# Output projection's inputs split by groups beside the last input projection, and gate and up products issued in turns

## The chip, the cores and the metric

The kernel runs on one core of a Trainium2 chip. TensorE (PE) multiplies matrices and also loads the stationary operand (PEld); VectorE (DVE), ScalarE (ACT) and GpSimd (POOL) do elementwise work; transfers from and to device memory are issued by SyncE (SP), a few by ACT and POOL, and run on 16 DMA engines. The metric is the device time of one execution in microseconds; lower is better. Each engine works through its own queue in order.

## The reference

One block of a diffusion transformer over 512 tokens of width 1024, with 256 context tokens, all in float32. Cut to what the change touches:

```python
def token_mix(h, w_in_l, w_out_l, ...):
    q, zf_f, zf_b, i, g, gate_b, gate_c, v = split_proj(h @ w_in_l)       # w_in: 1024 x 4096
    o_hg, s_f, s_b = hgrn2_mix(q, i, zf_f, zf_b, g, ...)                  # 4 heads, normalised, times silu(g)
    u = gate_c * v
    y = gate_b * dwconv3(u, conv_l)                                       # 3 taps along the grid row
    return jnp.concatenate([o_hg, y], axis=-1) @ w_out_l, s_f, s_b        # w_out: 1024 x 1024

def expert_choice_ffn(h, w_router, w_gate, w_up, w_down):                 # 16 experts, 64 tokens each
    aff = jax.nn.softmax(h @ w_router)
    gate, idx = lax.top_k(aff.T, cap)
    xs = h[idx]
    hid = silu(xs @ w_gate) * (xs @ w_up)                                 # 1024 -> 2048, per expert
    return zeros.at[idx].add((hid @ w_down) * gate)                       # 2048 -> 1024

def reference(...):
    x = x + g1 * mx            # mx: output of token_mix
    hx2 = modulate(rms_norm(x, norm_ffn), sh2, sc2)
    x = x + g2 * expert_choice_ffn(hx2, ...)
    return rms_norm(x, norm_final)
```

## The kernel before

It has three stages. **Input projections and heads**: the 1024 x 4096 projection runs section by section. Since the plain float32 product is slow, each operand is split into a rounded part (hi, made by ACT) and a rest (lo, made by DVE), and three products are summed: hi*hi, hi*lo, lo*hi (`split_w` L264, `products` L286). Between the sections the four recurrent heads are worked off (`scores`, `head_sum`, `head_gate`). The result, 1024 features by 512 tokens, stands in `mixed`: four rows of 128 features from the heads (k = 0 to 3, written by `head_gate` L576) and four from the convolution (k = 4 to 7, written by `keep_gb` L599). The last section is the second half of `gate_b`; its last product feeds `keep_gb(3)`, and `head_gate(3)` follows it.

**Output projection and routing**: `out_weights` (L754) loads `w_out` in four pieces of 1 MB (columns 0 to 511 and 512 to 1023, features 0 to 511 and 512 to 1023), multiplies the second column half by `g1b` on POOL (L761) and splits each piece into `wo_hi` (ACT, L764) and `wo_lo` (DVE, L765). `mix_parts` (L747) splits `mixed` for one block of 128 tokens into `m` (ACT L751, DVE L752). `residual` (L783) multiplies one token block by one column half: 24 matmuls (L792 to L794), for k = 0 to 7 hi*hi, hi*lo, lo*hi. Then come the sum with x, a transpose (L805), the router's logits (L810), and for each block the softmax and the running top 64 of each expert (`affinity`, `top`), the last of it on DVE alone.

**Experts**: 16 experts in 8 pairs. Each expert's `w_gate` and `w_up` come in 8 pieces each of 1 MB (128 rows by 2048), each pair's two `w_down` in 16. 64 tokens fill only half of PE's columns, so the gate products write to rows 0 to 63 of a PSUM bank and the up products to rows 64 to 127 (`hidden` L969, matmuls L979); four banks `gu` hold 2048 columns. Each float32 matmul of the program is two in the trace, and so four pairs per piece are 16 matmuls of L979 in the trace. After them the banks are copied (L989), transposed (`ht`, L994), multiplied into `hid` (L998), and go through `w_down` (`y`, L1033), the gates (L1005) and the scatter (`po`, L1011). Weights are streamed through `ring_a` (4 slots of 1 MB; the pieces of `w_in` and `w_out` go through it too) and, from the third stage on, 13 more (`ring_b`) and four lent ones. A load is issued in the program's order on SP and waits until the matmuls that read its slot are done; up to eight loads are under way at a time.

The order on each engine is set by the Tile scheduler, which places what is ready by the program's order, or earlier by `tc.high_priority(offset=300)` (300 instructions earlier in rank); `tc.issue_after(ins)` puts what the block traces on the engine of `ins` behind `ins` in its queue, without a wait for it to end. In the program so ordered, ACT's queue behind the last head's small steps holds: `wo_hi` of columns 512 to 1023 (first piece), `wo_hi` of columns 0 to 511 (both), `m` for the four token blocks, `wo_hi` of columns 512 to 1023 (second piece). The first of these is written over `h_hi`, which the last projection's matmuls read. PE's queue holds the gate and up products of expert 0 in turns (gate, up, gate, up, ...); from the middle of expert 1 on it holds, piece by piece, the eight gate products in a row and then the eight up products; of 512 gate products of the program 73 are followed at once by the up product of the same bank.

Tiles of a stage are laid over those of stages that are over, and each waits for the last reader of what lies under it. `wo_hi` of columns 0 to 511 lies over the heads' buffers, `wo_lo` over the heads' buffers with the last head's normalised output `on` and the begin of `vtok`, `m_0` and `m_1` over the rest of `vtok`, the states and the queries; `m_2`, `m_3` and the second column half over `sig`, `h_hi`, `h_lo` and the split weights.

## Time and profile before

| | |
|---|---|
| median of 3 runs | 1326.99 us (1326.15 to 1328.63) |
| profiled execution | 1325.83 us, of which the span is 1324.0 us |
| instructions | 15074 |
| PE busy | 1259.7 us (95%) |
| DVE, ACT, POOL busy | 407.2, 231.4, 42.6 us |
| read from device memory | 455.73 MB, 346 GB/s over the span |
| chain that ended last | PE 85%, issue 9%, DVE 4%, ACT 2%, DMA 1% |

The profile is one execution. A row of the timeline has the start, the duration, the engine, the line, the operation, what is written from what is read, and a count; in brackets stands how long the engine stood idle before it and what ended that. Rows of windows give, for each stretch, its length, the busy time of each engine with its number of instructions, the granted TensorE clock (1.00 is 2.4 GHz, 0.50 is 1.2 GHz), the share of the DMA engines and GB/s. A busy PE isn't PE at its peak: matmuls overlap, and a row merges neighbours of one kind.

### The profile page before, as it was taken

The numbers are of one execution on the slowest core, as the hardware profiler recorded it, in microseconds if no ns is written. First come the engines' busy times: TensorE is split into PE (matmuls) and PEld (weight loads), VectorE is DVE, ScalarE is ACT, GpSimd is POOL, SyncE is SP. The second block draws the span as 40 slices with busy tenths as digits, with TensorE's granted clock in tenths as the row PEclk, the third lists the DMA queues.
The fourth block names the chain that finished last, engine by engine and source line by source line (L and its number), as shares of the span: only waits on it lengthen the run. The fifth ranks groups of instructions, "written<-read, shape, count | busy, mean of one in ns | idle before, by whom it ended". The sixth has DMA issues, their size and how long they took to land.

```text
span 1324.0 us, 15074 instructions
## 1 busy us (share of the span) xinstructions
PE 1259.7 (95%) x6250; PEld 680.4 (51%) x6250; DVE 407.2 (31%) x843; ACT 231.4 (17%) x473; POOL 42.6 (3%) x47
## 2 busy tenths in 40 slices
PE   5999999998969999999999999999999999999995
PEld 3688988876834344444444444444444444444432
DVE  5557667885452111112111111211121121011113
ACT  4422554524311000000100000010000001000012
POOL 1000031140000000000000000000000000000000
PEclk9999999998979999999999999999999999999998
DMA  9567622218389999999999999999999999999993
GB/s 370 205 224 258 207 76 89 71 38 312 142 356 398 407 427 373 412 426 427 427 426 427 426 427 426 426 427 427 427 426 427 426 427 427 426 427 426 424 407 133
DMA packets 94608, 458.83 MB, mean 347 GB/s; under 512 B 7245, under 2 KB 21690, under 8 KB 47434
## 3 DMA queue, kind: packets, MB, share of 16 engines
q1 hardware_dynamic: 93360, 454.06, 84.1%
q0 software_dynamic: 992, 3.74, 0.8%
q8 instruction: 49, 0.80, 0.2%
q14 instruction: 21, 0.17, 0.0%
q10 hardware_dynamic: 186, 0.06, 0.0%
HBM read 455.73 MB, written 2.10 MB: 346 GB/s over the span
## 4 chain that ended last, share of the span: by engine, by line
PE 85%; issue 9%; DVE 4%; ACT 2%; DMA 1%; POOLq 0%; DVEq 0%; POOL 0%; ACTq 0%
PE gu L979 36%; PE y L1033 15%; PE pg L937 5%; PE px L290 3%; PE px L291 3%; PE px L295 3%; PE po L1011 3%; PE ht L994 2%; PE wo L792 1%; PE wo L794 1%; PE wo L793 1%; PE pi L406 1%; PE pi L407 1%; PE pi L405 1%; PE px_f L324 1%
## 5 line engine op out<-in xcount | busy, mean ns | idle before, releaser
L979 PE MATMUL gu<-wg,shared 128*64 128x512 f32 x1024 | 465.8, 600 | 0.7 <-ACT gs L989 0.7
L979 PE MATMUL gu<-wu,shared 128*64 128x512 f32 x1024 | 462.8, 599 | 0.0
L1033 PE MATMUL y<-wd,hid 128*64 128x512 f32 x896 | 209.2, 595 | 0.0
L979 PEld LDWEIGHTS gu<-wg,shared 128*64 128x64 f32 x1024 | 127.5, 136 | 154.6 <-issue 149.1
L979 PEld LDWEIGHTS gu<-wu,shared 128*64 128x64 f32 x1024 | 128.7, 136 | 136.0 <-issue 135.2
L1033 PEld LDWEIGHTS y<-wd,hid 128*64 128x64 f32 x896 | 81.4, 137 | 112.1 <-issue 108.5
L989 DVE COPY gs<-gu 128x512 f32<-128x512 f32 x32 | 22.0, 691 | 321.0 <-PE gu L979 321.0
L937 PEld LDWEIGHTS pg<-pool_a,x 128*128 128x128 f32 x512 | 62.4, 195 | 40.7 <-issue 35.0
L1005 DVE SCALAR_TENSOR_TENSOR yt<-y,gate,g2b 128x512 f32<-128x512 f32 x16 | 12.0, 750 | 217.2 <-PE y L1033 193.4
L290 PE MATMUL px<-h_hi,whi 128*128 128x512 f32 x192 | 76.9, 400 | 0.0
L989 ACT COPY gs<-gu 128x512 f32<-128x512 f32 x32 | 18.7, 587 | 331.7 <-PE gu L979 331.7
L295 PE MATMUL px<-h_hi,wlo 128*128 128x512 f32 x192 | 75.3, 392 | 0.0
L291 PE MATMUL px<-h_lo,whi 128*128 128x512 f32 x192 | 74.9, 390 | 0.0
L937 PE MATMUL pg<-pool_a,x 128*128 128x128 f32 x512 | 71.8, 289 | 1.6 <-DVE pool_a L929 1.6
L940 ACT ACTIVATE shared<-pg,b,a 128x128 f32<-128x128 f32 x32 | 14.6, 458 | 295.9 <-PE pg L937 295.9
L943 DVE TENSOR_SCALAR shared<-pg,a,b 128x128 f32<-128x128 f32 x32 | 13.1, 410 | 132.1 <-PE pg L937 132.1
L283 DVE TENSOR_TENSOR wlo<-wi,whi 128x1024 fp32r<-128x1024 f32 x28 | 38.8, 1384 | 27.0 <-ACT whi L282 27.0
L1011 PE MATMUL po<-yhl,g 128*128 128x512 f32 x128 | 40.4, 427 | 5.9 <-ACT yhl L1006 5.9
L1006 ACT CAST yhl<-yt 128x512 fp32r<-128x512 f32 x16 | 9.9, 618 | 193.3 <-DVE yt L1005 193.3
L1011 PEld LDWEIGHTS po<-yhl,g 128*128 128x128 f32 x128 | 21.5, 188 | 41.4 <-ACT yhl L1006 13.8
L608 DVE SCALAR_TENSOR_TENSOR adas<-wa,shared,adas 128x512 f32<-128x512 f32 x56 | 41.4, 747 | 1.4 <-DMA wa<-in_w_ada 0.4
L994 PE MATMUL ht<-ident,gs 128*128 128x128 f32 x256 | 34.9, 279 | 6.9 <-DVE hid L998 6.9
(315 smaller groups left out, 1326.1 us busy)
## 6 DMA issues: line engine op xcount, KB each, us to landing
wg<-in_w_gate SPq DMA_DIRECT2D x128, 1024.0 KB, 18.4
wu<-in_w_up SPq DMA_DIRECT2D x128, 1024.0 KB, 15.6
wd<-in_w_down SPq DMA_DIRECT2D x120, 1024.0 KB, 15.3
wa<-in_w_ada SPq DMA_DIRECT2D x22, 1024.0 KB, 6.5
wi<-in_w_in SPq DMA_DIRECT2D x16, 1024.0 KB, 5.2
wd<-in_w_down SPq DMA_DIRECT2D x16, 512.0 KB, 10.4
wo<-in_w_out SPq DMA_DIRECT2D x4, 1024.0 KB, 5.3
xt<-in_x SPq DMA_DIRECT2D x2, 1024.0 KB, 6.7
```

The lines of the kernel that those rows point to most:

```text
L283: dve.tensor_tensor(lo, v, hi.bitcast(F32), op=ALU.subtract)
L290: mm(px, hi[:, k], h_hi[:, k], start=f, stop=False)
L291: mm(px, hi[:, k], h_lo[:, k], start=False, stop=False)
L295: mm(px, lo[:, k], h_hi[:, k], start=False, stop=l)
L608: dve.scalar_tensor_tensor(acc, ts[k // 4][:, (k % 4) * 512:(k % 4 + 1) * 512], cs[:, k, 0:1], acc, op0=ALU.mult, op1=ALU.add)
L937: mm(pg[:, :P], x1[:, tb, k * P:(k + 1) * P], ohr[:, tb], start=tb == 0, stop=tb == NT - 1)
L940: act.activation(xs[:, k], pg[:, :P], AF.Identity, scale=a2[:, k, 0:1], bias=b2[:, k, 0:1])
L979: mm(gu[n][i * CAP:(i + 1) * CAP], xs[:, k, ssl], w[:, n * 512:(n + 1) * 512], start=k == 0, stop=k == KD - 1, skip_group_check=True)
L989: (act.copy if n % 2 else dve.tensor_copy)(to, fr)
L994: pe.transpose(pt[:, i * P:(i + 1) * P], gs[:, f * P:(f + 1) * P], ident)
L1011: mm(po, g[:, tb * P:(tb + 1) * P], yhl[:, i, nsl], start=first and i == 0, stop=i == 1)
L1033: mm(y[n][i * CAP:(i + 1) * CAP], hid[:, i, f], wd[i][:, s, n * 512:(n + 1) * 512], start=f == 0, stop=f == DFF // P - 1, skip_group_check ...
```

## The change

It has three parts.

1. The inputs of the output projection. `mix_parts` and `out_weights` are ranked 300 instructions earlier for token block 0 and columns 0 to 511, and block 0 is split by groups of k: 0 to 2, 4 to 6, then 3 and 7, so that the first two need neither `head_gate(3)` nor `keep_gb(3)`. `head_gate(3)` is ranked earlier too. The second `wo_lo` piece is queued behind `keep_gb(3)` on DVE. Token blocks 1 to 3 follow, and the casts of columns 512 to 1023 are queued on ACT behind the last cast of `m`. In the first `residual` the 24 matmuls are ordered by the groups: hi*hi and lo*hi of k 0 to 2, hi*lo of these, then hi*hi and lo*hi of the other groups, and hi*lo of those last.
2. The tiles' places. On the left side the order was `wo_hi`, `wo_lo`, `m_0`, `m_1`; it becomes `wo_hi`, `m_0`, `m_1`, `wo_lo`. So `m_0` lies over the heads' buffers, `m_1` over `on` and the begin of `vtok`, and `wo_lo` over `vtok`, states and queries.
3. Gate and up products. Each L979 product is queued behind the one before it in the program's order, through all experts, so they go gate, up, gate, up.

The same sums are made from the same products; in the first `residual` they are added in another order.

```diff
     def keep_gb(i, px):
-        dve.tensor_tensor(cy[i], cy[i], px, op=ALU.mult)
+        mixed_last.append(dve.tensor_tensor(cy[i], cy[i], px, op=ALU.mult).ins)
...
-    head_gate(HEADS - 1)
+    with tc.high_priority(offset=PRIO):
+        head_gate(HEADS - 1)
...
+    groups = [slice(0, 3), slice(4, 7), slice(3, 8, 4)]
+
+    def mix_parts(tb, ks):
         src = mixed[:, ks, tb * P:(tb + 1) * P]
-        act.copy(mix[tb][:, 0, ks], src)
+        ins = act.copy(mix[tb][:, 0, ks], src)
         dve.tensor_tensor(mix[tb][:, 1, ks], src, mix[tb][:, 0, ks].bitcast(F32), op=ALU.subtract)
+        return ins
+
+    def out_weights(n, q):
+        raw = stream(w_out[0, q * 512:(q + 1) * 512, n * 512:(n + 1) * 512]
+                     .rearrange("(k p) n -> p k n", p=P), f"wo_{n}_{q}")
+        rv = raw.rearrange("p (k n) -> p k n", k=4)
+        if n:
+            gp.tensor_tensor(rv, rv, g1b[:, n * 512:(n + 1) * 512].unsqueeze(1)
+                             .to_broadcast([P, 4, 512]), op=ALU.mult)
+        hi, lo = (t[:, 4 * q:4 * q + 4] for t in wo[n])
+        act.copy(hi, rv)
+        return lambda: dve.tensor_tensor(lo, rv, hi.bitcast(F32), op=ALU.subtract)
...
+    wo[0] = [p_out.tile([P, KD, 512], F32R, name="wo_hi_0")]
+    for tb in range(NT):
+        mix[tb] = (p_out if tb < 2 else late).tile([P, 2, KD, P], F32R, name=f"m_{tb}")
+    wo[0].append(p_out.tile([P, KD, 512], F32R, name="wo_lo_0"))
+    wo[1] = [late.tile([P, KD, 512], F32R, name=f"wo_{q}_1") for q in ("hi", "lo")]
+    with tc.high_priority(offset=PRIO):
+        rest = [out_weights(0, 0)]
+        for g in groups[:2]:
+            mix_parts(0, g)
+        rest.append(out_weights(0, 1))
+        mix_parts(0, groups[2])
+        rest[0]()
+        with tc.issue_after(mixed_last[-1]):
+            rest[1]()
+    for tb in range(1, NT):
+        ready = mix_parts(tb, slice(0, KD))
+    with tc.issue_after(ready.ins):
         for q in range(2):
...
-    out_weights(0, p_out)
-    for tb in range(NT):
-        mix_parts(tb, slice(0, KD), p_out if tb < 2 else late)
-    out_weights(1, late)
+            out_weights(1, q)()
...
-        for k in range(KD):
-            hi, lo = mix[tb][:, 0, k], mix[tb][:, 1, k]
-            mm(po, hi, whi[:, k, nsl], start=k == 0, stop=False)
-            mm(po, hi, wlo[:, k, nsl], start=False, stop=False)
-            mm(po, lo, whi[:, k, nsl], start=False, stop=k == KD - 1)
+        hi, lo = mix[tb][:, 0], mix[tb][:, 1]
+        three = [(hi, whi), (hi, wlo), (lo, whi)]
+        if tb == 0 and c == 0:
+            a, b, d = ([*range(KD)[g]] for g in groups)
+            steps = [(w, k) for ks in (a, b, d) for w in three[::2] for k in ks]
+            steps = steps[:6] + [(three[1], k) for k in a] + steps[6:] + [(three[1], k) for k in b + d]
+        else:
+            steps = [(w, k) for k in range(KD) for w in three]
+        for i, ((m, wt), k) in enumerate(steps):
+            mm(po, m[:, k], wt[:, k, nsl], start=i == 0, stop=i == len(steps) - 1)
...
+    pairwise = []
...
                 for i, w in enumerate((wg, wu)):
-                    mm(gu[n][i * CAP:(i + 1) * CAP], xs[:, k, ssl], w[:, n * 512:(n + 1) * 512],
-                       start=k == 0, stop=k == KD - 1, skip_group_check=True)
+                    with tc.issue_after(pairwise[-1]) if pairwise else nullcontext():
+                        ins = mm(gu[n][i * CAP:(i + 1) * CAP], xs[:, k, ssl],
+                                 w[:, n * 512:(n + 1) * 512], start=k == 0, stop=k == KD - 1,
+                                 skip_group_check=True)
+                    pairwise[:] = [ins.ins]
```

## Rows read from the trace of the kernel before

**Rows 1.** The page: the GB/s that the DMA engines moved in 40 slices of the span, and one line of the DMA issues (count, KB each, median us from issue to landing).

```profile
GB/s 370 205 224 258 207 76 89 71 38 312 142 356 398 407 427 373 412 426 427 427 426 427 426 427 426 426 427 427 427 426 427 426 427 427 426 427 426 424 407 133
...
wg<-in_w_gate SPq DMA_DIRECT2D x128, 1024.0 KB, 18.4
```

**Rows 2.** One pair of experts in the middle of the third stage, from the scatter of one pair to that of the next (606.31 to 722.75): windows of all engines, windows of the L979 products alone, and two pieces of the chain that ended last (start, us, what) inside it.

```profile
606.31:722.75 116.44, 114.82 (x508) 49.84 (x508) 18.79 (x43) 9.07 (x19) 0.00 (x0) 1.00 1.01 427
...
606.31:722.75 116.44, 67.13 (x256) 23.25 (x256) 1.00 1.01 427
...
623.60 5.35 PE gu L979 x16
...
637.38 16.00 PE gu L979 x64
```

**Rows 3.** Expert 0, whose gate and up products go in turns: a window of L979 alone for one piece of each (k = 1), and three of its rows on PE's timeline.

```profile
389.88:393.46 3.58, 3.58 (x16) 1.05 (x16) 1.00 0.93 339
...
391.64 0.59 PE L979 MATMUL gu<-wg,shared 128*64 128x512 f32 x1
391.65 0.59 PE L979 MATMUL gu<-wu,shared 128*64 128x512 f32 x1
392.07 0.59 PE L979 MATMUL gu<-wg,shared 128*64 128x512 f32 x1
```

**Rows 4.** PE's timeline from the last input projection to the output projection.

```profile
295.58 0.39 PE L553 MATMUL o<-s_c,q2d 128*128 128x128 f32 x2
...
301.29 0.60 PE L575 MATMUL pt_o<-ident,on 128*128 128x128 f32 x4
308.04 0.79 PE L792 MATMUL wo<-wo_hi,m 128*128 128x512 f32 x1 [6.15 <-ACT m L751]
```

**Rows 5.** ACT's timeline in that stretch.

```profile
296.01 0.28 ACT L559 ACTIVATE on<-o 128x128 f32<-128x128 f32 x1 [10.46 <-PE o L553]
...
301.54 5.50 ACT L764 CAST wo_hi<-wo 128x2048 fp32r<-128x2048 f32 x3 [3.82 <-PE px L295]
306.95 3.88 ACT L751 CAST m<-mixed 128x1024 fp32r<-128x1024 f32 x4
```

**Rows 6.** DVE's timeline in that stretch.

```profile
298.62 0.69 DVE L568 TENSOR_TENSOR on<-o,or 128x512 f32<-128x512 f32 x1
301.49 0.69 DVE L599 TENSOR_TENSOR mixed<-mixed,px 128x512 f32<-128x512 f32 x1 [2.18 <-PE px L295]
...
303.47 6.69 DVE L765 TENSOR_TENSOR wo_lo<-wo,wo_hi 128x2048 fp32r<-128x2048 f32 x3 [0.70 <-ACT wo_hi L764]
310.09 4.62 DVE L752 TENSOR_TENSOR m<-mixed,m 128x1024 fp32r<-128x1024 f32 x4
```

**Rows 7.** Windows of all engines around the begin of the output projection (after the window and its length: PE, PEld, DVE, ACT, POOL, clock, DMA share, GB/s).

```profile
301.90:308.04 6.14, 0.00 (x0) 0.00 (x1) 5.44 (x5) 6.14 (x5) 0.00 (x0) 0.88 0.35 106
308.04:313.23 5.19, 5.19 (x11) 3.50 (x12) 5.19 (x4) 4.59 (x4) 0.00 (x0) 0.50 1.01 384
313.23:318.50 5.27, 5.27 (x24) 4.37 (x23) 4.53 (x5) 0.00 (x0) 0.00 (x0) 0.99 0.60 197
```

**Rows 8.** SP's timeline: the last load of `w_in`, and the second and third of `w_out`; and ACT's first cast of that last `w_in` piece.

```profile
211.62 0.37 SPq L70 DMA_DIRECT2D wi<-in_w_in  x1
...
244.47 15.88 SPq L70 DMA_DIRECT2D wo<-in_w_out  x2
...
265.47 1.04 ACT L282 CAST whi<-wi 128x1024 fp32r<-128x1024 f32 x1 [1.24 <-PE px L291]
```

**Rows 9.** Windows in the first two pairs of experts in which the DMA engines moved less (columns as in rows 7), and the SP queue's longest total wait from 420 to 600 (us in total, times, longest).

```profile
425.00:435.00 10.00, 10.00 (x56) 4.40 (x54) 2.05 (x8) 1.35 (x3) 0.00 (x0) 1.00 0.83 306
515.00:530.00 15.00, 15.00 (x58) 5.69 (x58) 1.81 (x8) 0.46 (x1) 0.00 (x0) 1.00 0.88 315
545.00:550.00 5.00, 5.00 (x24) 2.01 (x22) 0.00 (x0) 0.00 (x0) 0.00 (x0) 1.00 0.91 351
...
SPq L70 <- PE gu L979: 102.4, 48, 11.1
```

**Rows 10.** The end: windows of 4 us (columns as in rows 7), and PE's timeline from the last up product on.

```profile
1284.00:1288.00 4.00, 4.00 (x20) 1.29 (x18) 0.00 (x0) 0.00 (x0) 0.00 (x0) 1.00 1.05 408
...
1296.00:1300.00 4.00, 4.00 (x17) 1.24 (x18) 3.02 (x5) 1.45 (x4) 0.00 (x0) 1.00 0.33 126
...
1267.57 2.31 PE L979 MATMUL gu<-wu,shared 128*64 128x512 f32 x5
...
1275.19 15.67 PE L1096 MATMUL y<-wd,hid 128*64 128x512 f32 x72
...
1297.30 10.51 PE L1096 MATMUL y<-wd,hid 128*64 128x512 f32 x46
```

**Rows 11.** The beginning of the kernel, where PE works in short bursts: windows of 2 us (columns as in rows 7), and PE's timeline there.

```profile
18.00:20.00 2.00, 1.12 (x5) 0.33 (x4) 0.69 (x1) 1.73 (x2) 0.00 (x0) 1.00 1.05 409
...
26.00:28.00 2.00, 0.89 (x2) 0.79 (x3) 1.21 (x4) 1.66 (x3) 0.00 (x0) 0.66 1.05 409
...
19.75 1.02 PE L215 MATMUL ada_t<-sel,ada_ev 128*128 128x2 f32 x8 [0.88 <-ACT whi L332]
...
27.11 2.08 PE L324 MATMUL px_f<-h_hi,whi 128*128 128x512 f32 x4 [2.22 <-ACT h_hi L309]
```

More of the change, by code (lines that the diff above doesn't have):

```diff
@@ L1 @@
-from contextlib import ExitStack
+from contextlib import ExitStack, nullcontext
 import concourse.bass as bass
@@ L596, in keep_v @@
                                  op0=ALU.mult, op1=ALU.add)
+    mixed_last = []
     def keep_gb(i, px):
-        dve.tensor_tensor(cy[i], cy[i], px, op=ALU.mult)
+        mixed_last.append(dve.tensor_tensor(cy[i], cy[i], px, op=ALU.mult).ins)
     def ada_sum(col0):
@@ L745, in dit_block @@
     mix, wo = {}, {}
-    def mix_parts(tb, ks, pool=None):
-        if pool:
-            mix[tb] = pool.tile([P, 2, KD, P], F32R, name=f"m_{tb}")
+    groups = [slice(0, 3), slice(4, 7), slice(3, 8, 4)]
+    def mix_parts(tb, ks):
         src = mixed[:, ks, tb * P:(tb + 1) * P]
-        act.copy(mix[tb][:, 0, ks], src)
+        ins = act.copy(mix[tb][:, 0, ks], src)
         dve.tensor_tensor(mix[tb][:, 1, ks], src, mix[tb][:, 0, ks].bitcast(F32), op=ALU.subtract)
-    def out_weights(n, pool):
-        wo[n] = [pool.tile([P, KD, 512], F32R, name=f"wo_{q}_{n}") for q in ("hi", "lo")]
-        for q in range(2):
-            raw = stream(w_out[0, q * 512:(q + 1) * 512, n * 512:(n + 1) * 512]
-                         .rearrange("(k p) n -> p k n", p=P), f"wo_{n}_{q}")
-            rv = raw.rearrange("p (k n) -> p k n", k=4)
-            if n:
-                gp.tensor_tensor(rv, rv, g1b[:, n * 512:(n + 1) * 512].unsqueeze(1)
-                                 .to_broadcast([P, 4, 512]), op=ALU.mult)
-            hi, lo = (t[:, 4 * q:4 * q + 4] for t in wo[n])
-            act.copy(hi, rv)
-            dve.tensor_tensor(lo, rv, hi.bitcast(F32), op=ALU.subtract)
@@ L767, in dit_block @@
-    late = tc.alloc_tile_pool(name="late", bufs=1, side="right", reuse_waits="tile")
-    out_weights(0, p_out)
-    for tb in range(NT):
-        mix_parts(tb, slice(0, KD), p_out if tb < 2 else late)
-    out_weights(1, late)
+        return ins
[9 more added lines that the diff above has]
+        return lambda: dve.tensor_tensor(lo, rv, hi.bitcast(F32), op=ALU.subtract)
@@ new lines, in dit_block @@
+    late = tc.alloc_tile_pool(name="late", bufs=1, side="right", reuse_waits="tile")
+    wo[0] = [p_out.tile([P, KD, 512], F32R, name="wo_hi_0")]
[12 more added lines that the diff above has]
+            rest[1]()
```

## The prediction

> **What bounds the kernel now.** First the 40 slices of the span with their GB/s [rows 1]: from the 17th slice on the DMA engines move 426 to 427 GB/s, slice after slice, but before the 13th much less. So the kernel has a first part, where transfers have time, and a second that is a stream of weights. In the second I read one pair of experts [rows 2]. Its period is 116.44 us; PE is busy for 114.82 of it, but the DMA share is 1.01. A pair needs 48 loads of 1.0486 MB (16 gate, 16 up, 16 down), 50.33 MB; at 427 GB/s that is 117.9 us. Both engines are full, and PE's work can't start before its weights land: the transfers are the bound there, PE only just behind. In the first part I read PE's idle time. The largest stretch on PE's own path is the 6.15 us before the first matmul of the output projection, put down to an ACT cast of `m` [rows 4].
>
> **Part 1, the inputs of the output projection.** ACT has nothing to do from 297.72 on (the end of its last row before the gap) and waits 3.82 us for the last projection's product, because the head of its queue, a cast of columns 512 to 1023, is written over `h_hi`; then come three casts of 1.83 each, and only then the cast of `m` at 306.95 [rows 5]. PE could have gone on at 301.9 [rows 4]. After the idle time the granted clock is 0.50 (1.2 GHz): 11 matmuls take 5.19 us, where 24 at 0.99 take 5.27, .22 each [rows 7]. So the cold start costs 5.19 − 11 × .22 = 2.8, and the most that this part can give is 6.15 + 2.8 = 8.9.
>
> What has to be ready. The heads' last product ends at 295.97 [rows 4], so from then on the new places are free; the normalised `on` is written until 299.31 [rows 6], but the tiles of block 0 no longer lie over it. ACT from 297.72: two casts of 1.83, and block 0's `m` (0.97 whole [rows 5], an estimated 1.2 in three parts) make 4.9, to about 302.6; the third part must wait for the two last multiplications, done near 303. DVE from 299.31, where a first `wo_hi` of 1.83 is just there: `wo_lo` 2.23 (6.69 / 3), the multiplications 2 × .69, the parts of `m` an estimated 1.4 (1.16 whole), the second `wo_lo` 2.23, together 7.2, to about 306.5 [rows 6]. PE, starting at 301.9, needs 24 × .22 = 5.3, to 307.2; its order puts the four products that read the second `wo_lo` last, at 306.3. DVE is therefore the tight engine. I put down 1.6 us: some .3 there, up to .6 for the last group, about .7 for block 1, whose DVE part comes at 307.7, and for `wo_lo` of columns 512 to 1023, which is now behind the rest. Gain 8.9 − 1.6 = 7.3. Bounds: 8.9, if nothing waits; about 4, if PE begins near 304.3 and cold again (6.15 − 2.4 = 3.7).
>
> Edits with one answer: the same casts are made, one in three parts (ACT and DVE have the spare time above). The loads of `w_out` are issued earlier on SP and may pass `w_in` there; before, the last `w_in` load is issued at 211.62 and first cast at 265.47, and the next but one `w_out` load at 244.47 [rows 8]: over 50 us of cover against the 18.4 from issue to landing of a load of this size [rows 1]. I cost that at nothing; without the cover it would be such a landing. POOL's multiplications stay with columns 512 to 1023. What is queued behind the added orders: on DVE the second `wo_lo` stands behind the last `gate_b` product, which it must let pass anyway; on ACT the casts of columns 512 to 1023 stand behind the last `m`, near 306 to 307, as against 301.54 and 310.74 for first and last before [rows 5]; the products that read them come after two blocks, 48 × .22 = 10.6 us behind 301.9.
>
> **Part 3, gate and up products.** Rows 0 to 63 and 64 to 127 of a bank are different columns of PE: in turns, the two start .01 us apart and the next gate product .43 after the first [rows 3]. A piece of both then takes 3.58 [rows 3]. In blocks a lone piece takes 5.35, and 64 in a row 16.00, or 4.00 a piece [rows 2]: some up products there run beside gate products of later pieces. Over a pair L979 takes 67.13 for 16 pieces, 4.20 each [rows 2]. All in turns: 16 × 3.58 = 57.3, which is 9.8 less, and PE's period falls from 116.4 to about 106.6, 11.3 below the 117.9 of the transfers.
>
> So the gain is not 8 × 9.8 = 78: it is what the transfers allow. It comes in two places. **Gaps of the stream.** In the first pairs SP's loads wait for PE to release slots (102.4 us in 48 waits; some do no harm, as up to eight loads run at once), and the engines move 306, 315 and 351 GB/s in three windows [rows 9]. Against 427 these lose 10 × 121/427 = 2.8, 15 × 112/427 = 3.9, and 5 × 76/427 = .9, together 7.7. The first is inside expert 0, which has turns already; the other two, 4.8, lie in the blocky part. I take 4, with 0 (another wait keeps the slots) and 7.7 as ends. **The end.** In the window 1296 to 1300 the engines move 126 GB/s x 4 us; at 407 that is 1.24 us, so the last weights land at 1297.24. PE's last down products end at 1307.8, 10.5 later [rows 10]: 46 matmuls, more than the last pieces need. With 10 us less per pair PE has long caught up, and only the last piece's 8 matmuls, .22 each, stand behind the landing: some 2 us. That gives 10.5 − 2 = 8.5. Against it: the last expert's own sequence. Its gate and up products end at 1269.8, its down products begin at 1275.2 and need 128 × .218 = 27.9 with 2.9 of `po` between [rows 10], while the last 16 loads need 41 us: it catches up within about 1. I take 8; bounds 6.5 and 8.6. What follows the last product stays.
>
> One rule speaks against this. What the rows show: PE, once it has caught up, waits about 4.91 − 3.58 = 1.3 us for each piece pair (2 loads / 427 GB/s). Early in the kernel PE works in bursts with waits of .24 to .88, busy 56% to 89%, at clock 1.00; a wait of 2.22 ends at clock .66 and then .50 [rows 11]. By the rows the new waits lie between these, nearer the harmless ones. The Trainium skill, TensorE: Matmul & The Clock Gate, section "HAM oscillation — how this bites in real kernels", says that a kernel whose K-tiles are shorter than the wait for the next slice falls to the low clock and starts every K-tile cold. By that rule each piece would pay the cold start again; our trace has its short waits at full clock, and no run so far shows it here.
>
> **The rivals.**
> (a) *The conversions come late.* A tile of the new layout, or the queue's order, holds a first cast until the `gate_b` product is through; for: the same happened to the head of ACT's queue in before [rows 5]. PE restarts cold near 304.3: 3.7 instead of 7.3, giving about 1310.
> (b) *Turns are hidden by the transfers everywhere.* The gaps stay and the tail is set by something else; against: the 46 matmuls after the last landing are PE's own backlog [rows 10]. Only part 1 remains: 1318.5.
> (c) *The clock falls in PE's new waits.* It limits itself: a cold piece, 3.58 + 2.8 = 6.4, is longer than the 4.9 of its loads, so PE lags and no longer waits, and the clock comes back. It costs about one cold start at the end, and some of the tail: 1309 to 1312.
> (d) *Slower: turns make products wait in line.* PE now has no gate product of its own to put between the 16 `po` of the expert before, which are paced by DVE, and every product stands behind the last. The four banks must be copied before the next expert's first product. Up to 11.3 us of such waits per pair are free (117.9 − 106.6); beyond, each adds in full. At 15 us, 3.7 × 8 = 30, giving about 1306.5 + 30 + 12 (gaps and tail lost) = 1348. Against: DVE is busy for 18.8 of 116.4, ACT for 9.1 [rows 2].
> (e) *No change*: the order comes out as before: 1326.
>
> **How the numbers follow.** On the profiled execution, 1325.83: −7.3 − 4 − 8 = −19.3, so 1306.5. That execution lies 1.2 below the median; I add half, **1307.0**. Chances: forecast 62% (its own range 1300 to 1313, from 8.9 + 7.7 + 8.6 = 25.2 down to 4 + 2 + 6.5 = 12.5); (a) 14%, (b) 10%, (c) 9%, (d) 3%, (e) 2%. Range: **1300 to 1317**, which takes in (a) and (c) and leaves out (b), (d), (e). A measurement of this kernel can tell about 0.2%, 2.7 us, from no change: faster 0.92, same 0.04, slower 0.04.
>
> **What would show it.** Right: no 6 us idle before the first product of `wo_hi`, and clock 1.00 in the 5 us behind it; on ACT the casts of columns 0 to 511 before 302; L979 at 57 us per pair; PE waiting on the DMA engines from the third or fourth pair on; 427 GB/s between 515 and 550; the last product about 2 us behind the last landing. Wrong: the transfers no longer at 427 in the middle of the stream, a clock below 1.00 there, or a first `wo_hi` cast that still waits for the `gate_b` product.

## The result, and the profile after

| | before | changed |
|---|---|---|
| median of 4 runs | 1327.8 us (1326.15 to 1328.63) | 1312.36 us (1310.99 to 1314.64) |
| profiled execution, its span | 1325.83, 1324.0 | 1314.64, 1312.9 |
| PE busy | 1259.7 | 1246.4 |

The ratio is 0.9887, 95% interval 0.9869 to 0.9905: some 15 us faster. 20 were forecast. The parts of the forecast came out as 8.2 (7.3 said) for the front, about 1.6 (4 said) for the gaps of the stream, and 5.7 (8 said) for the end.

**A beginning that differs between executions.** The two profiles can't be laid over each other as they are. The next fences show, for the kernel before, the changed kernel, and the changed kernel's second profile (the first experiment below), first the transposes of the third head on PE's timeline, which stand ahead of everything that was changed (up to them each engine has the same instructions in the same order), and then the windows of 20 to 40 us.

```profile
278.34 0.66 PE L575 MATMUL pt_o<-ident,on 128*128 128x128 f32 x4 [0.29 <-DVE on L568]
```

```profile
20.00:30.00 10.00, 6.78 (x38) 4.28 (x39) 8.16 (x13) 4.22 (x8) 0.00 (x0) 0.83 1.05 412
30.00:40.00 10.00, 10.00 (x55) 5.70 (x53) 1.30 (x7) 1.71 (x3) 1.79 (x3) 1.00 1.05 403
```

```profile
282.65 0.66 PE L575 MATMUL pt_o<-ident,on 128*128 128x128 f32 x4 [0.30 <-DVE on L568]
```

```profile
20.00:30.00 10.00, 7.24 (x33) 3.54 (x33) 6.34 (x11) 2.63 (x5) 0.00 (x0) 0.55 1.04 411
30.00:40.00 10.00, 10.00 (x41) 6.25 (x40) 3.21 (x10) 3.16 (x6) 1.79 (x3) 0.76 0.99 386
```

```profile
280.49 0.66 PE L575 MATMUL pt_o<-ident,on 128*128 128x128 f32 x4 [0.30 <-DVE on L568]
```

```profile
20.00:30.00 10.00, 6.46 (x38) 4.39 (x39) 7.97 (x13) 4.61 (x7) 0.00 (x0) 0.77 1.05 412
30.00:40.00 10.00, 10.00 (x46) 6.25 (x46) 1.50 (x8) 2.04 (x5) 1.78 (x3) 0.89 1.01 385
```

The number to look at is the clock, the third from the end of each window row: 0.83 and 1.00, then 0.55 and 0.76, then 0.77 and 0.89; with it go the same transposes at 278.34, 282.65 and 280.49. The second and the third of these are one kernel in two executions, 2.2 us apart before anything that was changed begins. So I count from those transposes, here called T0. From T0 to the end of the span the kernel before takes 1324.0 − 278.34 = 1045.7 us, the changed kernel 1030.3 and, in its second profile, 1029.9: **15.4 to 15.8 us less**, close to what the medians show. All profiles below are compared in that way.

**The front.** PE's timeline, then ACT's, then DVE's, of the changed kernel around the begin of the output projection, and the two windows of all engines that answer to [rows 7].

```profile
306.33 0.84 PE L817 MATMUL wo<-wo_hi,m 128*128 128x512 f32 x3
307.65 0.96 PE L817 MATMUL wo<-wo_hi,m 128*128 128x512 f32 x3 [0.48 <-DVE m L756]
```

```profile
301.75 1.89 ACT L767 CAST wo_hi<-wo 128x2048 fp32r<-128x2048 f32 x1
303.54 0.92 ACT L755 CAST m<-mixed 128x384 fp32r<-128x384 f32 x2
304.36 1.91 ACT L767 CAST wo_hi<-wo 128x2048 fp32r<-128x2048 f32 x1
308.70 3.26 ACT L755 CAST m<-mixed 128x256 fp32r<-128x256 f32 x4 [2.42 <-DVE mixed L601]
```

```profile
304.24 0.69 DVE L576 TENSOR_TENSOR mixed<-pt_o,mixed 128x512 f32<-128x512 f32 x1 [0.81 <-PE pt_o L575]
304.85 2.28 DVE L768 TENSOR_TENSOR wo_lo<-wo,wo_hi 128x2048 fp32r<-128x2048 f32 x1
307.05 1.02 DVE L756 TENSOR_TENSOR m<-mixed,m 128x384 fp32r<-128x384 f32 x2
307.98 0.68 DVE L601 TENSOR_TENSOR mixed<-mixed,px 128x512 f32<-128x512 f32 x1
308.58 2.29 DVE L768 TENSOR_TENSOR wo_lo<-wo,wo_hi 128x2048 fp32r<-128x2048 f32 x1
```

```profile
302.00:308.00 6.00, 5.25 (x25) 3.81 (x24) 4.98 (x10) 4.28 (x4) 0.00 (x0) 1.00 0.80 322
308.00:313.00 5.00, 5.00 (x23) 4.10 (x22) 5.00 (x6) 4.30 (x5) 0.00 (x0) 1.00 0.82 256
```

Of the 6.15 us [rows 4] one wait of 0.48 is left, on DVE's part of `m`, and the clock stays at 1.00 where it fell to 0.50 [rows 7]. ACT casts `wo_hi` while PE is still at the last projection, and the longer wait is now ACT's (2.42). The first gather of the experts, on PE's timeline of the kernel before and of the changed kernel:

```profile
381.63 3.64 PE L937 MATMUL pg<-pool_a,x 128*128 128x128 f32 x16 [1.63 <-DVE pool_a L929]
```

```profile
377.73 3.75 PE L960 MATMUL pg<-pool_a,x 128*128 128x128 f32 x16 [1.63 <-DVE pool_a L952]
```

From T0 that is 103.3 and 95.1: the front gave 8.2 us.

**One pair of experts.** Windows of the changed kernel from the scatter of one pair to that of the next, of all engines and of L1006 (before: L979) alone, as in [rows 2].

```profile
713.01:825.98 112.97, 111.52 (x508) 44.88 (x508) 18.72 (x43) 9.07 (x19) 0.00 (x0) 1.00 1.01 427
...
713.01:825.98 112.97, 61.18 (x256) 18.30 (x256) 1.00 1.01 427
```

The period is 112.97 against 116.44, and L1006 takes 61.18 against 67.13. Both fell, but by 3.5 and 5.9 us, where 9.8 were forecast. In PE's queue the scatter's products, the gather blocks and the transposes now stand, in places, between the gate and the up product of the same bank. Two pieces of the chain that ended last show what that costs: one product alone (two matmuls of the trace) and two side by side (four).

```profile
713.52 1.00 PE gu L1006 x2
...
717.06 1.01 PE gu L1006 x4
```

The lone one takes as long as the two. The transfers run at 427 GB/s as before.

**The end.** Windows of the last transfers of the kernel before, then of the changed kernel, with the last down products on PE's timeline.

```profile
1292.00:1294.00 2.00, 2.00 (x8) 0.63 (x7) 1.01 (x2) 0.23 (x1) 0.00 (x0) 1.00 1.05 404
1294.00:1296.00 2.00, 2.00 (x8) 0.76 (x6) 1.22 (x3) 1.11 (x4) 0.00 (x0) 1.00 0.71 277
1296.00:1298.00 2.00, 2.00 (x7) 0.59 (x8) 1.63 (x3) 0.72 (x2) 0.00 (x0) 1.00 0.53 199
1298.00:1300.00 2.00, 2.00 (x12) 0.65 (x10) 1.38 (x3) 0.72 (x2) 0.00 (x0) 1.00 0.14 54
...
1299.60:1299.80 0.20, 0.20 (x4) 0.04 (x2) 0.03 (x1) 0.00 (x0) 0.00 (x0) 1.00 0.05 20
1299.80:1300.00 0.20, 0.20 (x4) 0.08 (x2) 0.00 (x0) 0.00 (x0) 0.00 (x0) 1.00 0.00 0
```

```profile
1294.20:1294.40 0.20, 0.20 (x4) 0.00 (x0) 0.00 (x0) 0.00 (x0) 0.00 (x0) 1.00 0.06 21
1294.40:1294.60 0.20, 0.20 (x4) 0.00 (x0) 0.00 (x0) 0.00 (x0) 0.00 (x0) 1.00 0.00 0
```

```profile
1274.26 5.33 PE L1125 MATMUL y<-wd,hid 128*64 128x512 f32 x22 [0.33 <-DMA wd<-in_w_down]
...
1286.04 10.61 PE L1125 MATMUL y<-wd,hid 128*64 128x512 f32 x46
```

The stream doesn't stop at once, it runs out over some 6 us: 404, 277, 199, 54 GB/s. In the kernel before the last bytes come at 1299.8, and PE's last product ends at 1307.8 [rows 10], 8.0 later. In the changed kernel they come at 1294.4, and PE ends at 1296.65, 2.3 later. So the end gave 5.7. The changed kernel's PE has no wait for weights behind the one of 0.33 that ends at 1274.26: from there it works for 22.4 us without a gap, and the last piece lands as PE comes to it (46 products take 10.61 us, against 10.51 in the kernel before, where each piece was there well ahead of its use).

From T0 the last bytes come at 1021.5 and 1011.7, 9.8 earlier: 8.2 of the front, and 1.6, the rest, of the gaps. Windows from 100 to 300 us behind T0, of the kernel before and of the changed kernel, agree with that: 402 instead of 399 GB/s over 200 us is worth 1.4 us at 427.

```profile
378.34:578.34 200.00, 194.84 (x903) 85.73 (x904) 33.94 (x91) 18.09 (x37) 0.00 (x0) 0.98 0.97 399
```

```profile
382.65:582.65 200.00, 197.89 (x926) 79.78 (x923) 29.49 (x72) 18.09 (x37) 0.00 (x0) 1.00 0.98 402
```

### The profile page after: what moved, and what is told of

Same layout as the page of the kernel before. It is cut to its first block, busy times and chain, and to the rows that moved or that the text cites. A ratio compares the mean times of both kernels' runs of the same rounds, so it can differ in the third digit from the quotient of the medians.

```text
span 1312.9 us, 15086 instructions
## 1 busy us (share of the span) xinstructions
PE 1246.4 (95%) x6250; PEld 647.5 (49%) x6250; DVE 406.8 (31%) x845; ACT 232.0 (18%) x475; POOL 43.1 (3%) x47
## 4 chain that ended last, share of the span: by engine, by line
PE 57%; DMA 30%; issue 8%; DVE 3%; ACT 1%; SPq 0%; POOLq 0%; ACTq 0%; DVEq 0%; POOL 0%
PE gu L1006 19%; DMA wu<-in_w_up 16%; DMA wd<-in_w_down 12%; PE y L1062 7%; PE pg L960 4%; PE wo L817 3%; PE px L290 3%; PE px L291 3%; PE px L295 3%; PE po L1040 2%; DMA spare<-in_w_ada 1%; PE ht L1023 1%; PE pi L406 1%; PE pi L405 1%; PE pi L407 1%
## 5 line engine op out<-in xcount | busy, mean ns | idle before, releaser
L1006 PE MATMUL gu<-wu,shared 128*64 128x512 f32 x1024 | 457.2, 597 | 7.3 <-DMA wu<-in_w_up 7.3
L1006 PE MATMUL gu<-wg,shared 128*64 128x512 f32 x1024 | 461.9, 598 | 0.7 <-ACT gs L1018 0.7
L1006 PEld LDWEIGHTS gu<-wu,shared 128*64 128x64 f32 x1024 | 133.8, 137 | 244.9 <-issue 226.3
L1062 PE MATMUL y<-wd,hid 128*64 128x512 f32 x896 | 228.5, 597 | 2.6 <-DMA wd<-in_w_down 2.6
L1006 PEld LDWEIGHTS gu<-wg,shared 128*64 128x64 f32 x1024 | 131.9, 137 | 35.3 <-issue 29.7
L960 PE MATMUL pg<-pool_a,x 128*128 128x128 f32 x512 | 77.4, 294 | 1.6 <-DVE pool_a L952 1.6
L817 PE MATMUL wo<-wo_hi,m 128*128 128x512 f32 (+1 forms) x144 | 41.8, 377 | 0.5 <-DVE m L756 0.5
```

What stands on the lines that cost most here:

```text
L817: mm(po, m[:, k], wt[:, k, nsl], start=i == 0, stop=i == len(steps) - 1)
L960: mm(pg[:, :P], x1[:, tb, k * P:(k + 1) * P], ohr[:, tb], start=tb == 0, stop=tb == NT - 1)
L1006: ins = mm(gu[n][i * CAP:(i + 1) * CAP], xs[:, k, ssl], w[:, n * 512:(n + 1) * 512], start=k == 0, stop=k == KD - 1, skip_group_check=True)
L1062: mm(y[n][i * CAP:(i + 1) * CAP], hid[:, i, f], wd[i][:, s, n * 512:(n + 1) * 512], start=f == 0, stop=f == DFF // P - 1, skip_group_check ...
```

## The experiments

The times are medians; each job also ran the kernel before (1328.1, 1328.4 and 1327.8 us in the three jobs, which hold four experiments each, in the order of the table). The last column is the span of one profile, counted from T0.

| run | median, us | ratio to before, 95% | span from T0, us |
|---|---|---|---|
| before | 1327.8 | | 1045.7 |
| changed | 1312.36 | 0.9869 to 0.9905 | 1030.3 |
| e1_after_again | 1311.75 | 0.9866 to 0.9893 | 1029.9 |
| e2_front_only | 1319.35 | 0.9927 to 0.9952 | 1038.1 |
| e3_turns_only | 1318.29 | 0.9919 to 0.9946 | 1037.4 |
| e4_turns_late | 1313.75 | 0.9880 to 0.9907 | 1032.1 |
| e5_no_sum_before_y | 1310.98 | 0.9857 to 0.9887 | 1030.1 |
| e6_one_slot_less | 1314.57 | 0.9884 to 0.9917 | 1032.2 |
| e7_old_places | 1311.26 | 0.9861 to 0.9891 | 1030.3 |
| e8_whole_block | 1314.59 | 0.9885 to 0.9915 | 1033.9 |
| e9_gather_twice_1 | 1316.65 | 0.9903 to 0.9936 | 1035.8 |
| e10_gather_twice_4 | 1312.87 | 0.9872 to 0.9901 | 1030.2 |
| e11_sums_later | 1308.37 | 0.9841 to 0.9870 | 1026.5 |
| e12_casts_free | 1311.79 | 0.9869 to 0.9899 | 1029.9 |

The theory: three separate gains (the front shifts all that follows; the stream's last gap closes earlier; PE catches up with the stream at the end). The rivals: the turns are hidden by the transfers, or the turns give in every pair.

### The changed kernel again

No edit.

> The changed kernel once more, nothing edited. Its first profile is 4.3 us behind the kernel before already at 280 us (the transposes of the third head at 282.65 against 278.34), with clock 0.55 and 0.76 in the windows 20 to 30 and 30 to 40 us, where the kernel before has 0.83 and 1.00; no instruction there was changed. Theory: that is the execution and not the change; the median stays at 1311 to 1313, and a profile whose clock in these two windows is as in the kernel before has those transposes near 278.4 and a span near 1308.6. Rival: the change shifts the beginning; then the transposes stand at 282 to 283 again in every profile.

T0 came at 280.49, at neither of the two values named, with clocks between the two. That speaks for the theory (the same kernel, 2.2 us apart), and the spans from T0, 1030.3 and 1029.9, agree. The profiles of the other runs have T0 from 278.29 to 281.16, with nothing edited ahead of it.

### One half of the change at a time

The front alone:

```diff
-                    with tc.issue_after(pairwise[-1]) if pairwise else nullcontext():
-                        ins = mm(gu[n][...], xs[:, k, ssl], w[...], ...)
-                    pairwise[:] = [ins.ins]
+                    mm(gu[n][...], xs[:, k, ssl], w[...], ...)
```

> The output projection's new inputs and places, but gate and up products in the order that the scheduler gives them, as before. Theory (front, gaps and tail add up): the front alone gives some 8 us, because it shifts the begin of the experts and with it all transfers; the product of the last pair stays 10 us behind its last landing: 1319 to 1320 against a before of 1327 to 1328. Rival (the turns carry the gain, and the earlier front is eaten by transfers that start no earlier): within 2 us of before.

The turns alone, in the kernel before:

```diff
-                    mm(gu[n][...], xs[:, k, ssl], w[...], ...)
+                    with tc.issue_after(pairwise[-1]) if pairwise else nullcontext():
+                        ins = mm(gu[n][...], xs[:, k, ssl], w[...], ...)
+                    pairwise[:] = [ins.ins]
```

> The kernel before with gate and up products in turns, nothing else changed. Theory: 6.5 us at the end (last product 4 us instead of 10.5 behind the last landing) and about 1 in the gaps of the stream, 1320 to 1321; L979 takes 57 to 58 us per pair instead of 67, and the middle pairs keep their period of 117 to 118 us. Rival (turns are hidden by the transfers everywhere): 1327. Rival (each pair gains 9.8): 1250.

From T0 the front alone gives 7.6 and the turns alone 8.3, together 15.9; both at once give 15.4 to 15.8. The halves add up, and neither rival holds. (In the medians of that job they give 8.8 and 9.8, together 18.6, against 16.4 for both at once; the medians hold the differing beginnings, which the spans from T0 leave out.) In the front-only run the first gather comes 95.1 after T0, as in the changed kernel, and its last product 8.85 behind the last byte (1300.19 and 1291.35). With turns only the last product stands 2.3 behind the last byte (1299.86 and 1297.55), which comes 2.7 earlier from T0 than before. Three figures of the second expectation missed: L979 takes 61.18 per pair and not 57 to 58, the middle period is 112.95 and not 117 to 118, and the last product stands 2.3 and not 4 behind the last landing.

### Turns only at the end

```diff
-                    with tc.issue_after(pairwise[-1]) if pairwise else nullcontext():
+                    with tc.issue_after(pairwise[-1]) if pairwise and e >= 12 else nullcontext():
```

> The changed kernel with turns from expert 12 on only; experts 0 to 11 in the scheduler's order. Theory: between 560 and 1240 us the transfers are the bound, so turns are worth something only while gaps remain (about 1 us, before 560) and at the end; two pairs with 11 us of slack each are enough to take back a backlog of 10 us: 1312 to 1314, at most 1.5 above the changed kernel of the same job, with the last product about 4 us behind the last landing. Rival (turns are worth something in each pair): some 5 us or more above the changed kernel.

1.8 to 2.2 us more than the changed kernel from T0 (1.4 to 2.0 in the medians): over the 1.5 that were the bound, and far from 5. The last product is again 2.25 behind the last byte. So two pairs with turns suffice for the end, though only just: PE's first wait for a landing in the third stage ends at 1274.21. The windows of this run show where the rest is:

```profile
520.00:540.00 20.00, 19.51 (x96) 8.76 (x93) 4.28 (x12) 3.29 (x7) 0.00 (x0) 1.00 0.98 392
540.00:560.00 20.00, 20.00 (x92) 8.05 (x90) 0.00 (x0) 0.00 (x0) 0.00 (x0) 1.00 1.01 421
```

In the changed kernel both are at 425 (its rows stand further below). What turns give besides the end they give before 560 us, and in the middle nothing.

### What sets the end

```diff
-    for tb in range(NT):
-        mm(pos[tb], ident, acc[tb][:, 512:], start=True, stop=False)
...
-        scatter(po, tb, nsl, False)
+        scatter(po, tb, nsl, True)
```

> The changed kernel without the eight matmuls that put the sums of the earlier pairs into PSUM before the last down products (3.5 us of PE between the last gate and up products and the first of those; columns 512 to 1023 of the output lack these sums). Theory (the end is set by the last weights to land): the last bytes come 2.3 us before the last product, as in the changed kernel (1294.35 and 1296.65); without the eight matmuls PE begins 3.5 us earlier and waits for weights instead: within 0.5 us of the changed kernel, still about 2.3 behind the last byte. Rival (PE itself sets the end, the distance of 2.3 is chance): 2 to 3.5 us faster, and the last product less than 1 us behind the last byte.

1030.1 from T0 against 1030.3 and 1029.9: nothing. The last byte comes at 1291.9, the last product ends at 1294.2, 2.3 later as before. PE's waits for the last down weights grew from 0.33 to 3.05 us, as these rows of this run show:

```profile
1266.69 3.65 PE L1123 MATMUL y<-wd,hid 128*64 128x512 f32 x16 [1.57 <-DMA wd<-in_w_down]
1271.83 5.33 PE L1123 MATMUL y<-wd,hid 128*64 128x512 f32 x22 [1.48 <-DMA wd<-in_w_down]
```

With 3.5 us less on PE ahead of the first down product the end stays where it was: landings set it, not PE's work before them. Which landing is not told apart: behind the last wait PE works for 22.4 us without a gap in both runs, so the piece that lands there, some 20 us before the last byte, fixes the end as much as the last one does.

### What the gaps are

```diff
-NB = 13
+NB = 12
```

> The changed kernel with 12 instead of 13 slots of 1 MB in the second ring of weights. Theory (the gaps that stay, 2.7 us at 420 to 440 and 2.9 at 500 to 520, are loads that wait for PE to release a slot, whatever the order of the products): each of the stretches in which the loads wait (340 to 400, 420 to 440, 500 to 520) loses one load more, 1.0486 MB at 427 GB/s = 2.46 us, so 2.5 to 7.5 us slower, 1314 to 1319. Rival (the gaps come from PE's pace or from the transfers themselves, not from the number of slots): within 1 us of the changed kernel.

1.9 to 2.3 us from T0, 2.2 to 2.8 in the medians. The rival (under 1) falls, the theory's lower end is about met, but not its reasoning: I had counted one load for each stretch, and it is about one load, 2.46 us, in all. From 80 to 100 us behind T0 the engines move 350 GB/s where the changed kernel moves 396, which is 2.2 us; over the 200 us behind that both move 402. So a load that isn't there in the first stretch isn't missed again in the later ones. My reading: what counts is how far PE has released slots when the loads wait for it the last time. The next two runs test that.

```diff
-            for tb in range(NT):
-                mm(pg[:, :P], x1[:, tb, k * P:(k + 1) * P], ohr[:, tb], start=tb == 0, ...)
+            for _ in range(2 if p == 1 else 1):
+                for tb in range(NT):
+                    mm(pg[:, :P], x1[:, tb, k * P:(k + 1) * P], ohr[:, tb], start=tb == 0, ...)
```

> The changed kernel with the 32 gather matmuls of pair 1 of the experts made twice (the second run overwrites the first with the same values): 8 blocks of 1.09 us, 8.7 us more PE work, in the down products of pair 0 and in expert 2, all before 517 us. Theory (the last stretch in which loads wait for PE, 500 to 520, sets when the stream ends; before it PE is the bound): 8 to 8.7 us slower, 1320, with the whole delay in the GB/s between 490 and 530 and none later. Rival (loads wait for something other than PE's pace): under 2 us.

With `p == 4` in the place of `p == 1`:

> The same 32 matmuls made twice, but those of pair 4 (some 820 to 880 us). Theory (with products in turns PE has 11.3 us to spare in each pair of the middle): the 8.7 us vanish in PE's waits, within 0.5 us of the changed kernel, and the stream stays at 427 GB/s. Rival (PE's spare time is not to be had, because its waits for each piece and the transfers' run-ahead don't make up for it): 3 to 8 us slower.

The same work costs 5.5 to 5.9 us from T0 (4.3 to 4.9 in the medians) ahead of that point and nothing (1030.2) far behind it. The windows of the run with pair 1 doubled, 500 to 560 us:

```profile
500.00:520.00 20.00, 20.00 (x112) 10.05 (x110) 0.82 (x2) 0.64 (x2) 0.00 (x0) 1.00 0.86 331
520.00:540.00 20.00, 19.51 (x102) 8.73 (x100) 5.43 (x17) 3.31 (x8) 0.00 (x0) 1.00 0.95 374
540.00:560.00 20.00, 20.00 (x96) 6.67 (x94) 0.72 (x4) 0.41 (x1) 0.00 (x0) 1.00 0.97 390
```

In the changed kernel the three are 365, 425 and 425. The loss is where the theory has it, but reaches on to 560, and it is some 3 us less than the 8 to 8.7 forecast. By then PE, at less time for a piece than its two loads take, may have made good part of the delay; that this is the missing 3 us was not tested.

### The same point, used

```diff
+            if k > 3 and pending:
+                with tc.issue_after(pairwise[-1]):
+                    pending.pop(0)()
             for b in blocks[k]:
-                block(b)
+                with tc.issue_after(pairwise[-1]) if e and k else nullcontext():
+                    block(b)
...
-        for tb in range(NT):
-            for n in range(2):
-                ...                       # products with g, addition to acc
+        pending += [partial(add_pair, tb, p, g, yhl) for tb in range(NT)]
```

> The changed kernel with the sums of a pair (the 16 products of its gates, and the additions on DVE) queued behind the products of pieces 3 to 6 of the next pair's first expert, and the gather blocks queued one by one behind its pieces, instead of all ahead of its second piece. The same work, later. Theory (the point at which PE has released the slots of expert 2's first pieces sets the end of the stream): some 5 us of PE work move behind that point, the 2.9 us lost at 500 to 520 go, and the 2.7 at 420 to 440 stay: 2.5 to 3 us faster than the changed kernel, near 1309. Rival (the loss comes back in the next stretch, or the sums then hold up the copies of the next expert): within 0.7 us, or slower.

1308.37 us, 1026.5 from T0: 3.4 to 3.8 us faster than the changed kernel from T0, and the fastest kernel of the study. The windows of this run, and then those of the changed kernel:

```profile
500.00:520.00 20.00, 20.00 (x84) 8.36 (x84) 6.79 (x17) 0.46 (x1) 0.00 (x0) 1.00 1.01 428
520.00:540.00 20.00, 19.51 (x100) 8.00 (x98) 4.92 (x14) 3.26 (x7) 0.00 (x0) 1.00 1.01 426
```

```profile
500.00:520.00 20.00, 20.00 (x100) 8.56 (x98) 2.60 (x10) 1.00 (x3) 0.00 (x0) 1.00 0.94 365
520.00:540.00 20.00, 19.51 (x98) 7.94 (x96) 4.28 (x12) 3.29 (x7) 0.00 (x0) 1.00 1.01 425
540.00:560.00 20.00, 20.00 (x96) 6.75 (x94) 0.00 (x0) 0.00 (x0) 0.00 (x0) 1.00 1.01 425
```

365 GB/s over 20 us became 428: the 2.9 us are gone. The gate and up products take 61.9 of a pair here too, so it isn't their speed, it is the order. The gain is somewhat over the 2.5 to 3 forecast. The same 200 us as above, from 100 to 300 us behind T0, hold nearly all of it: 409 instead of 402 GB/s is worth 3.3 us.

```profile
378.29:578.29 200.00, 198.84 (x942) 81.39 (x940) 29.95 (x73) 18.06 (x37) 0.00 (x0) 1.00 0.98 409
```

The sums and the gather blocks were moved together; what each gives alone was not run.

### The parts of the front

The tiles in the old order:

```diff
+    wo[0].append(p_out.tile([P, KD, 512], F32R, name="wo_lo_0"))
     for tb in range(NT):
         mix[tb] = (p_out if tb < 2 else late).tile([P, 2, KD, P], F32R, name=f"m_{tb}")
-    wo[0].append(p_out.tile([P, KD, 512], F32R, name="wo_lo_0"))
```

> The changed kernel with the tiles of the output projection laid in the old order (wo_lo before m_0 and m_1, so that wo_lo lies over the normalised head and the begin of vtok). Theory: nothing, within 0.5 us; in the changed kernel's trace the first wo_lo begins at 304.85, behind the transposes of the normalised head, which end at 304.20, because DVE does the last head's multiplication first anyway. Rival (the places are needed): wo_lo waits, the first block's products wait for it, 1 to 4 us slower.

Nothing: 1030.3. In the present order of DVE's queue the places of the tiles are not needed.

Block 0 in one piece:

```diff
         rest = [out_weights(0, 0)]
-        for g in groups[:2]:
-            mix_parts(0, g)
         rest.append(out_weights(0, 1))
-        mix_parts(0, groups[2])
+        mix_parts(0, slice(0, KD))
```

> The changed kernel with block 0 of m converted in one piece behind both casts of columns 0 to 511, not by groups. Theory (the groups let PE go on at once): the cast of m waits for the last gate_b product's multiplication, which ends at 308.66 in the changed kernel, DVE's part follows, and the first product begins about 3.4 us later (309.7 instead of 306.3); the wait costs 3.4 and part of a cold start (up to 2.8): 3 to 6 us slower. Rival (the order on ACT, wo_hi ahead of everything that waits, is the whole gain): within 1 us.

3.6 to 4.0 us from T0. PE's timeline and a window of this run show the wait and the clock (0.88) that the groups take away:

```profile
304.97 1.45 PE L815 MATMUL wo<-wo_hi,m 128*128 128x512 f32 x4 [2.36 <-ACT m L755]
```

```profile
302.60:308.00 5.40, 2.46 (x8) 1.45 (x8) 5.40 (x5) 4.12 (x5) 0.00 (x0) 0.88 0.77 255
```

The first gather comes 99.9 after T0, 4.8 later than in the changed kernel; 3.6 to 4.0 of that reach the end. So of the 8.2 us of the front 4.8 are the groups, and the other 3.4 are what this run keeps, the order of the queues (with the groups in, the new places give nothing; without them they were not tried).

The casts of columns 512 to 1023 not held back:

```diff
-    with tc.issue_after(ready.ins):
-        for q in range(2):
-            out_weights(1, q)()
+    for q in range(2):
+        out_weights(1, q)()
```

> The changed kernel with the casts of columns 512 to 1023 not queued behind the last cast of m on ACT; the scheduler then puts the first of them ahead of the third part of block 0's m, where it waits for the last projection's matmuls to leave what it is written over (306.3 in the changed kernel). Theory: it fits between 306.3 and 308.7, where ACT waits for the last gate_b product's multiplication anyway (2.42 us idle, the cast takes 1.9): within 0.5 us of the changed kernel. Rival (it delays the m of blocks 0 and 1, and PE waits): 1 to 2 us slower.

1029.9: nothing, as expected. The cast goes into ACT's wait: it begins at 302.38 in this run, 1.90 long, and 0.26 is left of the wait.

## Why the prediction came out as it did

- **Right:** the sign, the three places, and that the transfers, not PE, say what the turns are worth: in the middle they give nothing (the runs with turns from expert 12 on, and with pair 4's gathers doubled).
- **The front, 7.3 forecast, 8.2 measured.** DVE is the tight engine, as said, and one wait of 0.48 is left. The 1.6 put down for waits were too much: the first group's wait, 0.48, is the only one that the trace shows on PE from 306 to 345 us. DVE took the second `wo_lo` behind the last `gate_b` multiplication at 308.58, just ahead of the products that need it. That the tiles had to move (the forecast counted on it for `m`) was not so. Nor did the loads of `w_out` pass those of `w_in`: up to T0 SP issues the same loads in the same order, so the cover that was costed at nothing was not needed. Casts held behind the last `m` on ACT cost nothing, as put down.
- **The gaps, 4 forecast, about 1.6 measured.** This step failed: it put the gaps of 515 to 550, 4.8 us, down to products in blocks. With all products in turns the changed kernel still loses 2.9 us at 500 to 520 (365 GB/s). What holds the slots back there is other work of PE ahead of the pieces of expert 2, sums and gathers: the run that moves them loses nothing there. And gaps were added up stretch by stretch, where, as the runs with one slot less and with doubled gathers suggest, it is how late the loads are at the last one that counts. The sign "427 GB/s between 515 and 550" held from 520 on (425), but not from 515 to 520 (308).
- **The end, 8 forecast, 5.7 measured.** The mechanism was right in the main (2 us behind the last weights forecast, 2.3 measured, and the run without the sums shows that landings set the end). That PE would catch up with the stream only within about 1 us was said too: its last wait ends 20 us before the last byte, and the last piece lands just as PE comes to it. The size was off because of the landing: 1297.24 came from the mean of one window of 126 GB/s, turned into full speed. The stream runs out over 6 us, and the last bytes came at 1299.8, 2.5 later, so that there were 8.0 to win and not 10.5.
- **PE's period, 106.6 forecast, 112.97 measured.** Too good by 6.4: pairs split by other work on PE's queue (61.18 against 57.3), and down products of 31.97 us per pair where they took 29.88; why these grew was not traced. It changed nothing in the sum, since what PE needs for catching up, 4.9 us per pair under 117.9, was there. But PE first waits for a landing at 935, not in the third or fourth pair.
- **The base.** The profiled execution of before lay 2 us below the later medians, not 1.2, so about 1.5 of the 5.4 us between forecast and median come from there, and 3.9 from the sum (19.3 forecast, 15.4 measured).

Of the rivals, (a) didn't occur (ACT's first cast of `wo_hi` begins at 301.75, and PE's last projection ends at 306.33), (b) fell with the turns-only run, (d) shows in its mechanism, products in line behind sums and transposes, at 6.4 us per pair, under the 11.3 from which it decides, and (e) is outside the interval. For (c): the clock did not fall, but the case that (c) describes, a wait at each piece, did not come about. The next rows are the only two waits for gate and up pieces in the pair from 939 to 1052, on the changed kernel's PE timeline; the window of all engines that they lie in follows.

```profile
1010.59 0.64 PE L1006 MATMUL gu<-wu,shared 128*64 128x512 f32 x1 [1.24 <-DMA wu<-in_w_up]
1015.49 0.64 PE L1006 MATMUL gu<-wu,shared 128*64 128x512 f32 x1 [1.24 <-DMA wu<-in_w_up]
```

```profile
939.00:1052.00 113.00, 108.53 (x490) 43.19 (x490) 18.13 (x42) 9.07 (x19) 0.00 (x0) 1.00 1.01 427
```

Two waits of 1.24 us, 4.47 us idle in all, and clock 1.00 throughout that window. The rule on K-tiles in the Trainium skill (TensorE: Matmul & The Clock Gate, "HAM oscillation — how this bites in real kernels") doesn't show here. It speaks of K-tiles shorter than the wait for the next slice; a piece takes 3.58 [rows 3] and the wait 1.24, so its condition isn't met, and it does not follow from it, as the prediction has it, that each piece would pay the cold start again.

The prediction's own reading of [rows 11], short waits harmless and one of 2.22 not, doesn't hold either. At the changed kernel's beginning the longest wait of PE from 14 to 40 us is the next one, shorter than 1.24, and yet the clock is 0.55 from 20 to 30 (the window above). So the length of a wait alone doesn't tell; what does was not tested.

```profile
29.18 2.08 PE L324 MATMUL px_f<-h_hi,whi 128*128 128x512 f32 x4 [1.01 <-ACT h_hi L309]
```

## What to carry to other kernels

Where transfers are the bound and loads wait for slots, look for the last stretch in which they wait: work of the engine that stands ahead of that point cost most of its time here (5.5 to 5.9 of 8.7 us), the same work far behind it nothing, so move what can wait past it. Take the last landing from windows of a fraction of a microsecond, not from the mean of one window. And count from an event ahead of the change when executions differ in their beginning.

## What was not expected of the hardware

- The clock early in the kernel differs between executions of one kernel: 0.55 and 0.76 in one, 0.77 and 0.89 in another (windows 20 to 30 and 30 to 40), and with it T0, by 2.2 us; over all profiles T0 goes from 278.29 to 282.65. Between the two profiles of the changed kernel that is 2.2 of the 2.5 us by which their spans differ.
- The last 6 us of a stream of 1 MB and 512 KB loads go from 404 GB/s to nothing by way of 277, 199 and 54 (the kernel before, windows of 2 us).
- A gate product whose up product isn't next in the queue takes as long as a pair (1.00 and 1.01): 61.18 us for 16 pieces, 3.82 each, with the queue in turns but with pairs split by other work, against 3.58 for a piece whose pairs are whole [rows 3].
